# Two heads share one product with the value columns in grouped attention

## The chip, the cores and the metric

The kernel runs on one core of a Trainium2 chip. The time is device microseconds of one execution on that core. The engines named here are TensorE (PE in the profile, with its weight loads as PEld), VectorE (DVE), ScalarE (ACT), GpSimd (POOL) and SyncE (SP); SP and POOL issue the DMA transfers of this kernel, apart from two stores that ACT issues.

## What is computed

Four decoder layers over 256 positions of width 2048, in the order latent attention, sparse attention, sliding-window attention, latent attention. Every layer also has four heads that attend to a memory of 256 rows, a SiLU gate over all head outputs, and one output projection that is added to the residual stream. Data is 32-bit floating point.

The sparse and the window layer are grouped: 32 query heads of 64 columns share 4 key/value heads, eight query heads to each. What the change touches is the last line of their attention, the weighted sum of the values:

```
s = jnp.einsum('bqgjd,bkgd->bgjqk', qb, kb, preferred_element_type=jnp.float32) * scale + bias
...
p = e / (jnp.sum(e, axis=-1, keepdims=True) + jnp.exp(sink - m))
return jnp.einsum('bgjqk,bkgd->bqgjd', p.astype(vb.dtype), vb)
```

These are the window layer's lines; the kernel computes the sparse layer in the same way, with the keys that a query does not select masked out of its weights, and without sinks. All eight query heads j of a group g are multiplied by the same 64 value columns.

## The kernel before

**Numbers in two parts.** A 32-bit operand is split into a high part, rounded to the type that TensorE multiplies, and a low part, the remainder (`split`, line 62: ACT writes the high part, DVE the low part). A product of two such operands is three products: high by high, high by low, low by high. Weights come from HBM through SP's queue into `wr`, are split into `wh` and `wl` (three buffers of each), and are multiplied by activations whose parts are already split. These splits are the bulk of ACT's and DVE's instructions.

**Layers and parts.** A layer's head outputs are made in six parts of 512 columns, in the order 4, 0, 1, 2, 3, 5 (line 844): parts 4 and 5 are memory heads, parts 0 to 3 self heads. In a grouped layer, a part is one key/value group g with its eight query heads. For each part, `project` multiplies the layer's input by the query columns and by the part's gate columns; `attend` runs the heads; the result `y`, gated and split, is multiplied by its rows of the output weights in `w_out` (line 827) one part later, after the next part's projections and attention have been stated.

**Order on the engines.** The program states the work part by part, and a scheduler fixes the order of instructions on each engine when the program is built, moving work of one part between that of another. So on TensorE the small products of a head stand between the large products `acc_q`, `acc_g` (query and gate projections) and `acc_wo` (output projection). Each engine then runs its own list in that order, and waits on semaphores for what other engines deliver.

**One head of a grouped layer** (`Grouped.attend`). Queries are in two blocks b of 128. Block 0 needs keys 0 to 127 only, block 1 all 256. TensorE makes the scores `sp` (lines 786 and 789); DVE adds the bias and takes the maximum (line 447); ACT takes the exponential `e` (line 452) and scales it by the reciprocal of the row sum; TensorE transposes the weights in three blocks of 128x128 into `ptp` (line 427): keys 0 by queries 0, keys 0 by queries 1, keys 1 by queries 1. `split` writes them as 128x384 tiles, the high part `pT` (two buffers) and the low part from the ring `hl` (`part_tile`, line 56, three buffers, which the query projection also uses before its transposes `tr`, line 395). Then come the weighted sums `o` (line 811), with the values `vz` as the stationary operand and the weights as the moving one: key block 0 with 256 columns (both query blocks), key block 1 with 128 columns (query block 1), each three times for the parts. That is six products for one head.

**Two heads in one tile of partitions.** A head has 64 output columns, a stationary operand 128. `vz` holds a group's 64 value columns between columns of zeros, so that an even head takes "values, zeros" and an odd head "zeros, values" and both add into the same 128 partitions of `o`. `o` has 512 columns: heads 0 and 1 of four fill columns 0 to 255, heads 2 and 3 columns 256 to 511. So heads 0 and 2 use the same stationary operand, and heads 1 and 3 the other. After four heads, DVE multiplies `o` by the gate into `yt` (line 415), and `split` writes it into `y`.

**Other users.** Memory attention and latent attention use the `pT` ring too. POOL issues the loads of a group's bias table `bm` (line 775) into a single buffer, and of the memory's keys and values.

Of the kernel before, what the change touches and what calls it, by code (L numbers as in the profile page):

```python
# [8 lines left out]
F32 = mybir.dt.float32  # L9
F32R = mybir.dt.float32r  # L10
# [5 lines left out]
P = 128  # L16
S = 256
# [7 lines left out]
MEMW = 1024  # L25
ST = 2
N_TAB = 384
PQ, AUX, WR = 5, 3, 5


@with_exitstack
def kernel(ctx: ExitStack, tc: tile.TileContext, a: dict, out: bass.AP,
# [13 lines left out]
    def tmp(name, n=512, dt=F32):  # L46
        return wk.tile([P, n], dt, name=name, tag=f"t{n}", bufs=3)
# [6 lines left out]
        return ap.bitcast(F32)  # L54

    def part_tile(dt=F32R):
        return wk.tile([P, 512], dt, name="hl", tag="hl", bufs=3)

    def copy_act(o, i, scale=1.0):
        nc.scalar.activation(o, i, AF.Copy, scale=scale)  # L60
# [1 line left out]
    def split(hi, lo, src):  # L62
        copy_act(hi, src)
        nc.vector.tensor_sub(lo, src, f32(hi))  # L64
# [348 lines left out]
    def gated(y, o, gT, j):  # L413
        yt = tmp("yt")
        nc.vector.tensor_mul(yt, o, gT[:, j:j + 2, :].rearrange("p a b -> p (a b)"))
        y3 = yt.rearrange("p (a b) -> p a b", a=2)
        split(y[:, 0, j:j + 2, :], y[:, 1, j:j + 2, :], y3)
# [73 lines left out]
    def memory_attend(nm, kT, v, qT, gT):  # L491
        y = act.tile([P, 2, 4, S], F32R, name="y", tag="y", bufs=2)
        for h in range(2):
            es = []
            mn, sm = small("mn", 2), small("sm", 2)
            for b in range(2):
                sp = misc("msp")
                qs = slice(b * P, (b + 1) * P)
                seq = [(qT[h][:, u, k, qs], kT[h][:, v_, k, :])
                       for k in range(2) for u, v_ in ((0, 0), (0, 1), (1, 0))]  # L500
                for n_, (l, r_) in enumerate(seq):
                    nc.tensor.matmul(sp[:, :S], l, r_, start=n_ == 0, stop=n_ == len(seq) - 1)
                nc.vector.tensor_reduce(mn[:, b:b + 1], sp[:, :S], AX.X, OP.max, negate=True)
                ms = small("ms", 2)
                nc.vector.tensor_mul(ms[:, :1], mn[:, b:b + 1], nm.col("rstd", b))
                e = wk.tile([P, S], F32, name="e", tag="e", bufs=4)
                nc.scalar.activation(e, sp[:, :S], AF.Exp, bias=ms[:, :1], scale=nm.col("rstd", b),
                                     accum_out=sm[:, b:b + 1])
                es.append(e)
            r = small("rc", 2)  # L510
            nc.vector.reciprocal(r, sm)
            for b in range(2):
                normalized(es[b], r[:, b:b + 1], S)
            tp = weights_T(es, [(0, 0), (1, 0), (0, 1), (1, 1)])
            pH, pL = (wk.tile([P, 512], F32R, name="pT", tag="pT", bufs=2) for z in range(2))
            split(pH, pL, tp)
            o = misc("mo")
            for j in range(2):
                c = (2 * h + j) * P
                seq = [(v[z][:, t, c:c + P], p_[:, t * S:(t + 1) * S])  # L520
                       for t in range(2) for z, p_ in ((0, pH), (0, pL), (1, pH))]
                for n_, (l, r_) in enumerate(seq):
                    nc.tensor.matmul(o[:, j * S:(j + 1) * S], l, r_, start=n_ == 0, stop=n_ == 5)
            gated(y, o, gT, 2 * h)
        return y
# [13 lines left out]
    class Latent:  # L539
# [6 lines left out]
        def first(self):  # L546
            nm, w, j = self.nm, self.w, self.j
            self.cT = [act.tile([P, 2, 4, S], F32R, name=f"cT{c}", tag=f"big{c}")
                       for c in range(4)]

            acc1 = rows_by(nm.at, 16, w, 0, (A_QL, 288), "kva")
            rows_ = act.tile([P, 2, 512], F32, name="ckv", tag="aux", bufs=AUX)
            for t in range(2):
                copy_act(rows_[:, t, :288], acc1[t][:, :288], scale=nm.col("rstd", t))
            acc2 = rows_by(nm.at, 16, w, 0, (A_QL + 288, 288), "kvb")
            ks = small("kss", 2, bufs=2)
            self.kr = act.tile([P, 2, S], F32R, name="kr", tag="kr", bufs=1)
            for t in range(2):
                copy_act(rows_[:, t, 288:], acc2[t][:, :224], scale=nm.col("rstd", t))
                square_sum(ks[:, t:t + 1], rows_[:, t, :])  # L560
                raw = wk.tile([P, S], F32, name="krw", tag="z", bufs=3)
                copy_act(raw[:, :A_ROPE], acc2[t][:, 224:288], scale=nm.col("rstd", t))
                kr = wk.tile([P, 1, A_ROPE], F32, name="krr", tag="krr", bufs=1)
                rope(kr, raw[:, None, :A_ROPE], t, 1)
                hl = wk.tile([P, 2, 2, A_ROPE], F32R, name="krh", tag="krh", bufs=1)
                for d in range(2):
                    split(hl[:, 0, d, :], hl[:, 1, d, :], kr[:, 0, :])
                transposed(lambda i0, i1: self.kr[:, i0:i1, t * P:(t + 1) * P],
                           [hl[:, v_].rearrange("p a b -> p (a b)") for v_ in range(2)])
            kvr = small("kvr", 2, bufs=3)  # L570
            rsqrt_mean(kvr, ks, A_KVL)
            for t in range(2):
                copy_act(rows_[:, t, :], rows_[:, t, :], scale=kvr[:, t:t + 1])
                to_features(self.cT[3], t, rows_[:, t, :], 56 + j * 4)

            sq = wk.tile([P, S], F32, name="cqs", tag="sco0", bufs=1)
            for c in range(6):
                acc = columns_by(nm.at, 16, w, 0, (c * 256, 256), "cq")
                for m in range(2):
                    n = 2 * c + m  # L580
                    z = total(acc[m])
                    s1 = sq if n == 0 else wk.tile([P, S], F32, name="cq1", tag="e", bufs=4)
                    nc.scalar.activation(s1, z, AF.Square)
                    if n:
                        nc.vector.tensor_add(sq, sq, s1)
                    gc = gvec[:, 32 + j * 12 + n:33 + j * 12 + n]
                    hi, lo = (self.cT[n // 4][:, v, n % 4, :] for v in range(2))
                    copy_act(hi, z, scale=gc)
                    nc.vector.scalar_tensor_tensor(lo, z, gc, f32(hi), op0=OP.mult, op1=OP.subtract)
            pr = misc("cqp")  # L590
            for t in range(2):
                nc.tensor.matmul(pr[:, t:t + 1], sq[:, t * P:(t + 1) * P], ones[:, :1], start=True, stop=True)
            s1 = small("cs1", 2)
            nc.vector.tensor_mul(s1, pr[:, :2], nm.rstd)
            s2 = small("cs2", 2)
            nc.vector.tensor_mul(s2, s1, nm.rstd)
            qn = small("qr", 2)
            rsqrt_mean(qn, s2, A_QL)
            qr = small("qx", 2)
            nc.vector.tensor_mul(qr, qn, nm.rstd)  # L600
            self.scale = small("qs", 2, bufs=2), small("qsn", 2, bufs=2)
            for z, sg in zip(self.scale, (1.0, -1.0)):
                nc.vector.tensor_scalar(z, qr, sg * (A_NOPE + A_ROPE) ** -0.5, None, op0=OP.mult)
# [31 lines left out]
        def attend(self, qn, qr, kn, v, gT):  # L635
            y = act.tile([P, 2, 4, S], F32R, name="y", tag="y", bufs=2)
            for h in range(4):
# [12 lines left out]
                        nc.tensor.matmul(sp[:, :S], l, r_, start=n_ == 0, stop=n_ == len(seq) - 1)  # L650
                    return sp
                tp = masked_softmax(score, lambda b, n: caus[:, S - n:], self.scale)
                pT = wk.tile([P, 512], F32, name="pT", tag="pT", bufs=2)
                copy_act(pT[:, :3 * P], tp[:, :3 * P])
                if h % 2 == 0:
                    o = misc("o")
# [7 lines left out]
    class Grouped:  # L664
# [113 lines left out]

        def attend(self, g, q, bm, gT):
            y = act.tile([P, 2, 4, S], F32R, name="y", tag="y", bufs=2)  # L780
            for h in range(8):
                def score(b):
                    sp = misc("sp")
                    qb = q[h // 4][:, h % 4, b * P:(b + 1) * P]
# [14 lines left out]
                    return bs[:, :n]  # L799
                nsk = None if self.sparse else nsink[:, g * 8 + h:g * 8 + h + 1]  # L800
                tp = masked_softmax(score, bias, None, nsk)
                pH, pL = wk.tile([P, 512], F32R, name="pT", tag="pT", bufs=2), part_tile()
                split(pH[:, :3 * P], pL[:, :3 * P], tp[:, :3 * P])
                if h % 4 == 0:
                    o = misc("o")
                c0 = (h // 2 % 2) * S
                v0 = g * P + (64 if h % 2 == 0 else 0)
                for t in range(2):
                    ks = slice(t * S, t * S + S - t * P)
                    for n_, (z, p_) in enumerate(((0, pH), (0, pL), (1, pH))):  # L810
                        nc.tensor.matmul(o[:, c0 + t * P:c0 + S], self.vz[z][:, t, v0:v0 + P], p_[:, ks],
                                         start=h % 2 == t == n_ == 0, stop=h % 2 == t == 1 and n_ == 2)
                if h % 4 == 3:
                    gated(y, o, gT, (h // 4) * 2)
            return y


# [121 lines left out]
```

## Time and profile before

| | |
|---|---|
| median of 3 runs | 2635.22 us (2634.94 to 2639.01) |
| the profiled execution | 2636.8 us, of which 2634.7 are the span of the trace |
| PE, weight loads, DVE, ACT, POOL busy | 2601.2, 2254.7, 1884.1, 1628.8, 57.3 us |
| granted TensorE clock | 0.997 of full speed |
| weighted sums of the sparse layer, first and last start on PE | 1175.5 and 1481.6 us |
| weighted sums of the window layer, the same | 1669.4 and 1974.8 us |

The rows of the timeline give start and length in us, engine, line, operation, the tiles written and read, the shape and the number of instructions that are merged into the row; in brackets the idle time before it and what ended it. Products on PE overlap, and their ends are modelled, so lengths add up to more than the time passed; distances between starts do not. Rows of a group (one line, operation and tile) give the count, the busy time, the mean in ns of one, and the idle time of the engine before them. Rows of the waits give the total, the number and the longest.

### The profile page before, as it was taken

What the parts mean: (1) busy time and instruction counts of PE and PEld (TensorE: products, weight loads), DVE (VectorE), ACT (ScalarE), POOL (GpSimd) and SP (SyncE); (2) the same over time, 40 slices, a digit from 0 to 9 for tenths busy, and PEclk for the clock granted to TensorE, in tenths of its full rate; (3) what the DMA queues carried; (4) which work ended last, traced back from release to release, by engine and by line L of the source; (5) the groups of instructions that cost most, each with busy time, mean ns of one, the idle gap of its engine ahead of it and who ended that gap; (6) DMA issues with size and microseconds to landing.
All of it is one profiled execution on the core that took longest, in us unless ns stands there. A gap on an engine that the chain in (4) does not pass through costs nothing.

```text
span 2634.7 us, 42943 instructions
## 1 busy us (share of the span) xinstructions
PE 2601.2 (99%) x14556; PEld 2254.7 (86%) x14556; DVE 1884.1 (72%) x4171; ACT 1628.8 (62%) x3476; POOL 57.3 (2%) x101
## 2 busy tenths in 40 slices
PE   8999999999999999999999999999999999999998
PEld 7888888888888889888888888888888888888886
DVE  6566656677767685877777776777778767776767
ACT  6455556556656566666666666676666655665655
POOL 1000000000000000000000000000000000000000
PEclk9999999999999999999999999999999999999999
DMA  9889886666557665555555555555555666655764
GB/s 305 279 287 300 281 256 198 166 185 168 169 160 224 192 192 172 167 183 170 173 163 191 188 190 177 173 172 178 189 168 162 205 165 186 165 170 156 226 183 135
DMA packets 456924, 511.70 MB, mean 194 GB/s; under 512 B 69584, under 2 KB 352480, under 8 KB 455552
## 3 DMA queue, kind: packets, MB, share of 16 engines
q1 hardware_dynamic: 443328, 451.75, 56.5%
q0 software_dynamic: 13088, 56.16, 6.6%
q8 instruction: 114, 1.87, 0.3%
q14 instruction: 106, 0.87, 0.1%
q10 hardware_dynamic: 288, 1.05, 0.1%
HBM read 489.91 MB, written 31.56 MB: 198 GB/s over the span
## 4 chain that ended last, share of the span: by engine, by line
PE 97%; DMA 1%; DVE 1%; ACT 0%; issue 0%; SPq 0%; ACTq 0%
PE acc_g L246 14%; PE acc_g L250 7%; PE acc_wo L227 7%; PE acc_wo L228 7%; PE acc_wo L229 7%; PE acc_mq L246 5%; PE acc_mk L246 5%; PE acc_qn L246 3%; PE acc_cq L246 3%; PE acc_mq L250 2%; PE acc_mk L250 2%; PE acc_q L227 2%; PE acc_q L228 2%; PE acc_q L229 2%; PE acc_mv L227 2%; PE acc_mv L228 2%
## 5 line engine op out<-in xcount | busy, mean ns | idle before, releaser
L64 DVE TENSOR_TENSOR wl<-wr,wh 128x512 fp32r<-128x512 f32 (+2 forms) x1776 | 1173.8, 664 | 645.1 <-ACT wh L60 614.2
L60 ACT ACTIVATE wh<-wr 128x512 fp32r<-128x512 f32 (+2 forms) x1776 | 1079.0, 609 | 837.3 <-PE acc_g L246 183.7
L246 PE MATMUL acc_g<-xT,wh 128*128 128x512 f32 x1536 | 489.0, 397 | 0.6 <-DVE z L257 0.6
L250 PEld LDWEIGHTS acc_g<-xT,wl 128*128 128x128 f32 x1536 | 285.2, 188 | 60.7
L250 PE MATMUL acc_g<-xT,wl 128*128 128x256 f32 x1536 | 311.0, 280 | 0.0
L228 PE MATMUL acc_wo<-wl,y 128*128 128x512 f32 x768 | 302.6, 394 | 0.6 <-DVE wl L64 0.5
L229 PE MATMUL acc_wo<-wh,y 128*128 128x512 f32 x768 | 299.1, 390 | 0.0
L246 PEld LDWEIGHTS acc_g<-xT,wh 128*128 128x128 f32 x1536 | 238.1, 189 | 4.8 <-issue 1.1
L227 PE MATMUL acc_wo<-wh,y 128*128 128x512 f32 x768 | 240.4, 393 | 0.7 <-ACT wh L60 0.6
L228 PEld LDWEIGHTS acc_wo<-wl,y 128*128 128x128 f32 x768 | 144.3, 188 | 30.0 <-DVE wl L64 1.4
L229 PEld LDWEIGHTS acc_wo<-wh,y 128*128 128x128 f32 x768 | 144.2, 188 | 28.4
L227 PEld LDWEIGHTS acc_wo<-wh,y 128*128 128x128 f32 x768 | 141.3, 188 | 27.8 <-ACT wh L60 1.0
L246 PE MATMUL acc_mk<-mT,wh 128*128 128x512 f32 x512 | 161.9, 398 | 2.4 <-ACT wh L60 2.4
L246 PE MATMUL acc_mq<-xT,wh 128*128 128x512 f32 x512 | 161.7, 397 | 0.0
L832 DVE TENSOR_TENSOR x<-x,acc_wo 128x512 f32<-128x512 f32 x192 | 125.7, 683 | 7.1 <-PE acc_wo L229 6.8
L246 PE MATMUL acc_qn<-cT,wh 128*128 128x512 f32 x384 | 123.2, 399 | 0.0
L246 PE MATMUL acc_cq<-xT,wh 128*128 128x512 f32 x384 | 120.8, 396 | 0.0
L250 PEld LDWEIGHTS acc_mk<-mT,wl 128*128 128x128 f32 x512 | 96.7, 189 | 23.4 <-DVE wl L64 0.8
L250 PEld LDWEIGHTS acc_mq<-xT,wl 128*128 128x128 f32 x512 | 93.7, 188 | 20.0
L250 PE MATMUL acc_mq<-xT,wl 128*128 128x256 f32 x512 | 102.5, 281 | 0.0
L228 PE MATMUL acc_q<-wl,xT 128*128 128x512 f32 x256 | 102.4, 400 | 0.0
L250 PE MATMUL acc_mk<-mT,wl 128*128 128x256 f32 x512 | 101.7, 280 | 0.0
(280 smaller groups left out, 4438.0 us busy)
## 6 DMA issues: line engine op xcount, KB each, us to landing
wr<-in_w_out_dram SPq DMA_DIRECT2D x192, 512.0 KB, 3.7
wr<-in_w_in_a_dram SPq DMA_DIRECT2D x176, 512.0 KB, 4.1
wr<-in_w_mem_kv_dram SPq DMA_DIRECT2D x128, 512.0 KB, 5.6
wr<-in_w_in_b_dram SPq DMA_DIRECT2D x112, 512.0 KB, 3.5
wr<-in_w_in_c_dram SPq DMA_DIRECT2D x104, 512.0 KB, 3.5
wr<-in_w_uq_dram SPq DMA_DIRECT2D x288, 128.0 KB, 2.6
tab<-flat POOLq DMA_DIRECT2D x8, 1536.0 KB, 11.1
wr<-in_w_in_a_dram SPq DMA_DIRECT2D x32, 288.0 KB, 3.0
```

The source lines that it names most:

```text
L60: nc.scalar.activation(o, i, AF.Copy, scale=scale)
L64: nc.vector.tensor_sub(lo, src, f32(hi))
L227: nc.tensor.matmul(acc[t][:, :n], xh, wh[:, :n], start=first, stop=False)
L228: nc.tensor.matmul(acc[t][:, :n], xh, wl[:, :n], start=False, stop=False)
L229: nc.tensor.matmul(acc[t][:, :n], xl, wh[:, :n], start=False, stop=last)
L246: nc.tensor.matmul(acc[j], wh[:, o:o + P], q[:, :, kt % 4, :], start=kt == 0, stop=False)
L250: nc.tensor.matmul(acc[j][:, 0, :], wl[:, o:o + P], q[:, 0, kt % 4, :], start=False, stop=kt == kts - 1)
L832: nc.vector.tensor_add(xs, xs, acc[t])
```

## The change

In `Grouped.attend` the heads run in the order 0, 2, 1, 3, 4, 6, 5, 7. The weights of two heads that have the same stationary operand (0 and 2, 1 and 3, and so on) are written side by side into one pair of tiles of 128x768, `pT2`, in the order key-and-query block, head, column. After the second head of a pair come its products: key block 0 with 512 columns (two query blocks of two heads), three times, and key block 1 with 256 columns (query block 1 of two heads), three times. `o` now holds its columns in the order query block, head, column, and the gating multiply reads it in that order. `o` is taken after the second head of a pair and not before the first.

Buffers: the `pT` ring has four tiles of 768 columns in place of two of 512, for memory and latent attention too; the `hl` ring has two tiles in place of three, and no longer holds the weights' low parts; the latent layer's `krh` shares the one buffer of `qrs`. The space on chip for descriptors of POOL's transfers is set to 8192 bytes of a partition; it was the default, 16384.

```diff
-PQ, AUX, WR = 5, 3, 5
+PQ, AUX, WR, PT = 5, 3, 5, 4
...
     def part_tile(dt=F32R):
-        return wk.tile([P, 512], dt, name="hl", tag="hl", bufs=3)
+        return wk.tile([P, 512], dt, name="hl", tag="hl", bufs=2)
...
-            pH, pL = (wk.tile([P, 512], F32R, name="pT", tag="pT", bufs=2) for z in range(2))
+            pH, pL = (wk.tile([P, 768], F32R, name="pT", tag="pT", bufs=PT)[:, :512] for z in range(2))
...
-                hl = wk.tile([P, 2, 2, A_ROPE], F32R, name="krh", tag="krh", bufs=1)
+                hl = wk.tile([P, 4, 2, A_ROPE], F32R, name="krh", tag="qrs", bufs=1)[:, :2]
...
-            for h in range(8):
+            for h in (0, 2, 1, 3, 4, 6, 5, 7):
...
-                pH, pL = wk.tile([P, 512], F32R, name="pT", tag="pT", bufs=2), part_tile()
-                split(pH[:, :3 * P], pL[:, :3 * P], tp[:, :3 * P])
-                if h % 4 == 0:
+
+                half, odd = h // 2 % 2, h % 2
+                if half == 0:
+                    pHL = [wk.tile([P, 3, 2, P], F32R, name="pT2", tag="pT", bufs=PT) for z in range(2)]
+                split(pHL[0][:, :, half, :], pHL[1][:, :, half, :],
+                      tp[:, :3 * P].rearrange("p (i c) -> p i c", i=3))
+                if half == 0:
+                    continue
+                if not odd:
                     o = misc("o")
-                c0 = (h // 2 % 2) * S
-                v0 = g * P + (64 if h % 2 == 0 else 0)
+                v0 = g * P + (0 if odd else 64)
                 for t in range(2):
-                    ks = slice(t * S, t * S + S - t * P)
-                    for n_, (z, p_) in enumerate(((0, pH), (0, pL), (1, pH))):
-                        nc.tensor.matmul(o[:, c0 + t * P:c0 + S], self.vz[z][:, t, v0:v0 + P], p_[:, ks],
-                                         start=h % 2 == t == n_ == 0, stop=h % 2 == t == 1 and n_ == 2)
-                if h % 4 == 3:
-                    gated(y, o, gT, (h // 4) * 2)
+                    for n_, (z, p_) in enumerate(((0, 0), (0, 1), (1, 0))):
+                        nc.tensor.matmul(o[:, t * S:], self.vz[z][:, t, v0:v0 + P],
+                                         pHL[p_][:, 2 * t:2 + t].rearrange("p i h c -> p (i h c)"),
+                                         start=odd == t == n_ == 0, stop=odd == t == 1 and n_ == 2)
+                if odd:
+                    j = (h // 4) * 2
+                    yt = tmp("yt")
+                    nc.vector.tensor_mul(yt.rearrange("p (j b c) -> p j b c", j=2, b=2),
+                                         o.rearrange("p (b j c) -> p j b c", b=2, j=2),
+                                         gT[:, j:j + 2, :].rearrange("p j (b c) -> p j b c", b=2))
+                    split(y[:, 0, j:j + 2, :], y[:, 1, j:j + 2, :], yt.rearrange("p (a b) -> p a b", a=2))
...
-    nc = _bacc.Bacc("TRN2", target_bir_lowering=False, num_devices=1)
+    nc = _bacc.Bacc("TRN2", target_bir_lowering=False, num_devices=1,
+                     dynamic_dma_scratch_size=8192)
```

More of the change, by code (lines that the diff above doesn't have):

```diff
@@ L652, in attend @@
                 tp = masked_softmax(score, lambda b, n: caus[:, S - n:], self.scale)
-                pT = wk.tile([P, 512], F32, name="pT", tag="pT", bufs=2)
+                pT = wk.tile([P, 768], F32, name="pT", tag="pT", bufs=PT)[:, :512]
                 copy_act(pT[:, :3 * P], tp[:, :3 * P])
```

## The prediction

> **What bounds the kernel now.** I read the page's first part, then the chain of work that ended last, then the groups of instructions of one line, the waits of TensorE, and last the timeline around the products that the change touches.
>
> ```profile
> span 2634.7 us, 42943 instructions
> PE 2601.2 (99%) x14556; PEld 2254.7 (86%) x14556; DVE 1884.1 (72%) x4171; ACT 1628.8 (62%) x3476; POOL 57.3 (2%) x101
> PE 97%; DMA 1%; DVE 1%; ACT 0%; issue 0%; SPq 0%; ACTq 0%
> 1240.00:1320.00 80.00, 79.23 (x433) 67.42 (x432) 60.85 (x149) 53.95 (x122) 0.89 (x1) 1.00 0.55 171
> 1750.00:1830.00 80.00, 79.53 (x437) 67.88 (x436) 60.65 (x152) 54.43 (x130) 0.89 (x1) 1.00 0.54 172
> ```
>
> TensorE (PE) is the chain for 97% of the span. The last two rows are busy time by stretch, one of the sparse layer and one of the window layer, each about one key/value group long (length, then PE, weight loads, DVE, ACT, POOL, then the granted clock, here 1.00). PE is busy over 79 of 80 us; DVE has 19 us and ACT 26 us to spare. So what the change does to DVE and ACT costs nothing unless it delays something PE waits for, and what it does to PE's stream shows in full.
>
> A busy PE is a modelled number, since the rows of one product overlap those of the next. What a product costs is the distance from its start to the next start:
>
> ```profile
> 1329.63 1.07 PE L227 MATMUL acc_wo<-wh,y 128*128 128x512 f32 x4
> 1330.54 0.39 PE L228 MATMUL acc_wo<-wl,y 128*128 128x512 f32 x1
> ...
> 1356.51 0.28 PE L811 MATMUL o<-pT,vz 128*128 128x256 f32 x1
> 1356.62 0.28 PE L811 MATMUL o<-hl,vz 128*128 128x256 f32 x1
> 1356.74 0.34 PE L811 MATMUL o<-pT,vz 128*128 128x256 f32 x2
> 1356.92 0.28 PE L811 MATMUL o<-hl,vz 128*128 128x128 f32 x1
> 1357.03 0.28 PE L811 MATMUL o<-pT,vz 128*128 128x128 f32 x1
> 1357.14 0.68 PE L227 MATMUL acc_q<-wh,xT 128*128 128x512 f32 x2
> 1357.66 0.40 PE L228 MATMUL acc_q<-wl,xT 128*128 128x512 f32 x1
> ```
>
> (Columns: start, length, engine, line, operation, tiles, shape, count.) Four products of 512 columns take 0.91 us, 0.228 each. A product of 256 columns takes 0.115 (1356.51 to 1356.74 is two); I use 0.117. One head's six products and two of 512 columns take 1.15 us; without the two (0.46) the head costs 0.69 us. Three products of 256 columns are 0.35 of that, so the three of 128 columns take 0.34, 0.11 each: as much as 256 columns. The last two starts, 1356.92 and 1357.03, show the same 0.11. That is the point of the whole case: below 256 columns a product here does not get cheaper, and 512 columns cost twice 256.
>
> **The change, part by part.**
>
> *The products.*
>
> ```profile
> L811 PE MATMUL o<-pT,vz 128*128 128x256 f32 (+1 forms) x256 | 53.4, 266 | 1.7 <-ACT pT L60 1.7
> L811 PE MATMUL o<-hl,vz 128*128 128x256 f32 (+1 forms) x128 | 35.6, 278 | 0.0
> ```
>
> 384 products, 64 heads of six, half of 256 and half of 128 columns: 64 x 0.69 = 44.2 us. Afterwards 32 pairs take three products of 512 and three of 256: 3 x 0.228 + 3 x 0.117 = 1.04 us, 33.2 us in all. The columns streamed are the same; what goes is 192 products and their weight loads, and the gain is that 128 columns paid for 256. The term is -11 us; with each step taken 0.01 us shorter or longer it is -10 to -12. All of it is on PE, so it counts in full. A line of the Trainium skill speaks against this: "TensorE: Matmul & The Clock Gate", Back-to-back issue gap, gives an isolated step of N/2.4 + 2.5 ns, 56 ns at 128 columns and 216 at 512; by it a pair would go from 990 to 975 ns and all pairs would save an estimated 0.5 us. The trace's 0.11 us at 128 columns denies it; it is nearer to the 107 ns that the same page's section on LDWEIGHTS gives for loading 128 columns.
>
> *Order, and the stalls around these products.*
>
> ```profile
> PE o L811 <- ACT pT L60: 1.7, 3, 0.6
> PE ptp L427 <- ACT e L60: 1.4, 3, 0.5
> ...
> 1223.58 0.38 PE L427 MATMUL ptp<-ident,e 128*128 128x128 f32 x2
> 1224.54 0.38 PE L811 MATMUL o<-pT,vz 128*128 128x256 f32 x1 [0.58 <-ACT pT L60]
> 1225.12 0.47 PE L246 MATMUL acc_g<-xT,wh 128*128 128x512 f32 x1 [0.20 <-DVE z L257]
> ...
> 1716.91 0.27 PE L811 MATMUL o<-pT,vz 128*128 128x128 f32 x1
> 1717.65 0.33 PE L427 MATMUL ptp<-ident,e 128*128 128x128 f32 x1 [0.46 <-ACT e L60]
> ```
>
> Three times in the sparse layer the transposes of a head's weights (L427) are followed on PE by the product that needs them; ACT must first copy them out. 0.96 us pass where two transposes need 0.22, then 0.58 where one product needs 0.12: 1.2 us, 3.6 for the three. Three times in the window layer the transposes come before the scaled weights are ready: 0.74 us instead of 0.11, 1.9 for the three. Together 5.5 us. The order of the changed program on each engine is fixed when it is built, so it can be read. Before, these three places have no product between:
>
> ```
> 6383 L427 Matmult ptp_13557<-ident_79,e_13551 128x128 x2
> 6384 L811 Matmult o_13488<-pT_13561,vz_12230 128x256
> ```
>
> Afterwards the fewest between a pair's last transposes and its first product is nine of 512 columns (2.1 us at 0.228), except for the very last pair, with five (1.1 us), where the order before has six. Between a head's last scores and its first transpose stands, with the steps above, 4.6 us of PE work where the window layer stalls for 0.62 us, so that 5.2 would have been enough; afterwards the least is 5.2, once in each layer, then 5.5. So by the order all six stalls go. I count 4.5 of the 5.5, leaving 1 us for a new one somewhere (one place of either kind above); the bounds are 0 and 5.5. Everything PE does before the sparse layer's first projection stands in the same order as before.
>
> *Weights side by side.* ACT and DVE write the same number of 128x384 tiles, now as three runs of 128 with gaps. Nearest rows, runs of 64 with gaps (qrs) against no gaps (mkT):
>
> ```profile
> L60 ACT ACTIVATE qrs<-qrr 128x256 fp32r<-128x256 f32 x16 | 6.5, 406 | 0.0
> L60 ACT ACTIVATE mkT<-zs 128x256 fp32r<-128x256 f32 x32 | 13.2, 413 | 6.1 <-DVE zs L352 6.0
> L415 DVE TENSOR_TENSOR yt<-o,gT 128x512 f32<-128x512 f32 x32 | 22.0, 688 | 4.0 <-PE o L811 4.0
> ```
>
> No cost: 406 against 413 ns. The gating multiply now reads its sums in runs of 128; were its 16 instructions in these layers twice as long, DVE would have 11 us more over eight groups, against 19 us free in each. The sums are read into y, which is multiplied by the output weights only after the next part's projections, so a later pair delays nobody.
>
> *Buffers.* The weights' ring grows from two tiles to four and the first head's tiles are held over two heads; the ring of 512-column tiles (hl) shrinks from three to two but loses the weights' low parts; a rotary temporary shares a buffer used later. Only hl can hurt: each tile is written by ACT and DVE and read by four transposes, and with two tiles ACT's write waits for the transposes of two tiles earlier, with weight splits queued behind it.
>
> ```profile
> L395 PE MATMUL tr<-identr,hl 128*128 128x128 f32 x196 | 23.0, 236 | 0.0
> ```
>
> 196 transposes are 49 tiles, no idle time before them. In the new order the least PE work between a tile's transposes and those two tiles later is 2.6 us, else 3.4 or more. ACT and DVE need 0.47 and 0.48 us for a half tile:
>
> ```profile
> L60 ACT ACTIVATE hl<-acc_q,x 128x256 fp32r<-128x256 f32 x32 | 14.9, 471 | 1.3 <-PE acc_q L229 0.7
> L714 DVE SCALAR_TENSOR_TENSOR hl<-acc_q,x,hl 128x256 fp32r<-128x256 f32 x32 | 15.1, 478 | 2.0 <-ACT hl L60 1.5 <-PE acc_g L250 0.6
> ```
>
> so about 1 us is needed where 2.6 is there. I take 0; the other end is a rival below.
>
> *POOL's descriptor space is halved.* Its queue issues the bias tables of a group:
>
> ```profile
> bm<-tab POOLq DMA_DIRECT2D x8, 1024.0 KB, 6.9
> ...
> 1306.28 0.89 POOL L775 DMA_DIRECT2D bm<-tab  x1 [79.31 <-DVE bs L798]
> 1322.71 0.29 DVE L798 TENSOR_TENSOR bs<-bm,vs 128x128 f32<-128x128 f32 x1
> ```
>
> Issued at 1306.3, landed 6.9 us later, first used at 1322.7: 9.5 us to spare. 0; were a load 10 us slower, each of eight groups would lose half a us.
>
> **Sum.** -11 - 4.5 = -15.5 us. The profiled execution took 2636.8 us for its span of 2634.7; the median of the runs is 2635.2, between the two. From the median: 2619.7, that is 0.6% faster.
>
> **The rivals.**
> 1. The products gain, the stalls don't go. They are where PE's filling work runs short, and the new order only moves that place, at the switch from one half of the gate to the other (the wait for z above) or beside the output products. For it: in this kernel they come back at the same place in each group. Against it: the distances above. 2635.2 - 11 = 2624.
> 2. A product's price goes by its columns, so that pairing changes nothing on PE, and only stalls go: 2635.2 - 4.5 = 2631, or 2634.7 if they stay. Against it: 0.11 us for 128 columns.
> 3. Slower: the two-tile hl ring. If ACT waits at each of 49 tiles and the wh splits behind it come late, PE stands still by the size of the stalls above, 0.6 us each: 29 us, 2635.2 + 29 - 15.5 = 2649. It decides from 15.5 / 49 = 0.32 us a tile. Against it: 2.6 us of PE work for 1 us of ACT and DVE, and no wait of PE on these transposes now.
>
> **Chances.** The forecast 0.61, rival 1 0.26, rival 2 0.06, rival 3 0.07. The measurement tells 0.2% (5.3 us) from no change. The forecast and rival 1 are both faster; rival 2 lies within 0.2% for most of its spread; rival 3 is slower. So faster 0.88, same 0.05, slower 0.07. The range takes in the forecast (2617 to 2623) and rival 1 (2622 to 2627), with the term of the products from -10 to -12 and that of the stalls from +1 to -5.5: 2616 to 2627.
>
> **What would show it.** Right: 192 products of L815, 96 of 512 and 96 of 256 columns, pairs of about 1.04 us from first start to last; a group's stretch about 1.9 us shorter than now, in the sparse and the window layer alike; no row of PE waiting for ACT's pT2 or e; waits before the sparse layer unchanged. Wrong: a step of 512 columns over 0.25 us with these weights; new PE waits on wh or wl in the two layers; DVE or ACT waiting for tr while PE is idle.

## The result and the profile after

The changed kernel takes 2616.65 us (median of 6 runs, 2613.39 to 2619.6); the kernel before takes 2636.04 us beside it (6 runs, 2634.39 to 2639.01). The ratio is 0.9925, with a 95% interval of 0.9912 to 0.9938: about 19.4 us faster, where 15.5 were forecast. The profiled execution took 2616.21 us. The first part of its page and its chain of work that ended last:

```profile
span 2614.0 us, 42540 instructions
PE 2586.5 (99%) x14364; PEld 2238.1 (86%) x14364; DVE 1882.5 (72%) x4171; ACT 1621.6 (62%) x3476; POOL 57.3 (2%) x101
PE 95%; DMA 2%; issue 1%; DVE 1%; ACT 1%; POOL 0%; SPq 0%; ACTq 0%; POOLq 0%
```

TensorE has 192 products fewer (14364 for 14556), still bounds the kernel, and is busy 14.7 us less; VectorE and ScalarE have as many instructions as before. The weighted sums by line and shape (count, busy us, mean ns, idle time before), then the timeline of one pair:

```profile
L815 PE MATMUL o<-pT,vz 128*128 128x512 f32 x96 | 32.6, 400 | 0.3 <-DVE pT L64 0.3
L815 PE MATMUL o<-pT,vz 128*128 128x256 f32 x96 | 16.6, 281 | 0.0
```

```profile
1352.87 1.22 PE L815 MATMUL o<-pT,vz 128*128 128x512 f32 x6
1353.92 0.63 PE L227 MATMUL acc_q<-wh,xT 128*128 128x512 f32 x2
1354.39 0.39 PE L228 MATMUL acc_q<-wl,xT 128*128 128x512 f32 x1
```

From the first product of the pair to the start of the third product behind it are 1.52 us; less two steps of 512 columns (0.46) the pair costs 1.06 us. The forecast was 1.04, and two heads before cost 1.38. The waits of TensorE after (total us, number, longest):

```profile
PE acc_mv L227 <- ACT wh L60: 9.4, 4, 8.4
PE acc_kvb L227 <- ACT wh L60: 2.7, 1, 2.7
PE acc_mk L246 <- ACT wh L60: 1.9, 2, 1.4
PE o L815 <- DVE pT L64: 0.3, 1, 0.3
PE acc_wo L228 <- DVE wl L64: 0.2, 1, 0.2
```

The three waits for ACT's `pT` and the three for `e` are gone. The new one of 0.3 us is at the very last pair. Before, TensorE also waited once at the end of the sparse layer and once at the end of the window layer for the output weights' splits (`acc_wo`, 0.6 and 0.5 us of idle time; the two rows are those quoted under experiment 4, which has them unchanged). Of that 0.2 us are left.

**Where the time went.** I divide every execution at two places, both before or behind everything the change touches on TensorE: the first product of the sparse layer's key/value projection (`acc_kv`) and the first of the last layer's (`acc_kva`). Between them lies what I call the grouped stretch. Busy time by that stretch, before and after (length, then PE, weight loads, DVE, ACT, POOL, granted clock, DMA share, GB/s):

```profile
977.77:2021.35 1043.58, 1038.57 (x5768) 894.17 (x5766) 784.26 (x1817) 682.06 (x1526) 19.07 (x27) 1.00 0.56 176
```

```profile
975.44:2000.71 1025.27, 1024.62 (x5576) 878.61 (x5574) 782.44 (x1817) 675.53 (x1526) 19.05 (x27) 1.00 0.57 180
```

The stretch is 18.3 us shorter. Behind it the two executions take the same time (2634.7 - 2021.35 and 2614.0 - 2000.71, both 613.3). Before it lie 2.3 us of difference (977.77 against 975.44), in a layer of which only buffers have changed. In the eleven profiles of this study the stretch begins between 975.4 and 980.9 us, and in the four other kernels whose head order or buffers alone differ (experiments 4 to 7) between 975.9 and 977.0. TensorE's waits there (the rows of `acc_mv`, `acc_kvb` and `acc_mk`) sum to 15.5 us before and 14.0 after, and to 17.1 in experiment 5 and 15.4 in experiment 7. I take the 2.3 us as a difference from run to run; the forecast that these waits stay as they were can't be judged more closely than that. The stretch is the better ruler for what follows: two kernels below whose edits did nothing came out at 1043.48 and 1043.52, within 0.1 us of the kernel before.

TensorE's idle time in the stretch fell from 5.0 to 0.65 us (length less busy time), its busy time by 13.95.

The rows that were forecast to stay as they were, splits of the weights and the gating multiply, after:

```profile
L60 ACT ACTIVATE pT<-ptp 128x384 fp32r<-128x384 f32 x64 | 31.2, 487 | 16.7 <-PE ptp L427 16.2
```

```profile
L64 DVE TENSOR_TENSOR pT<-ptp,pT 128x384 fp32r<-128x384 f32 x64 | 35.5, 555 | 2.8 <-ACT pT L60 2.8
L821 DVE TENSOR_TENSOR yt<-o,gT 128x512 f32<-128x512 f32 x16 | 11.0, 688 | 1.5 <-PE o L815 1.4
```

and the two splits before, where they wrote without gaps (ACT's high part, then DVE's low part):

```profile
L60 ACT ACTIVATE pT<-ptp 128x384 fp32r<-128x384 f32 x64 | 31.1, 486 | 20.5 <-PE ptp L427 20.0
```

```profile
L64 DVE TENSOR_TENSOR hl<-ptp,pT 128x384 fp32r<-128x384 f32 x64 | 35.5, 554 | 0.6 <-ACT pT L60 0.6
```

The multiply took 688 ns before too. Runs of 128 with gaps cost nothing.

### The profile page after: what moved, and what is told of

It is laid out like the page before. It is cut to its first block, busy times and chain, and to the rows that moved or that the text cites. A ratio compares the mean times of both kernels' runs of the same rounds, so it can differ in the third digit from the quotient of the medians.

```text
span 2614.0 us, 42540 instructions
## 1 busy us (share of the span) xinstructions
PE 2586.5 (99%) x14364; PEld 2238.1 (86%) x14364; DVE 1882.5 (72%) x4171; ACT 1621.6 (62%) x3476; POOL 57.3 (2%) x101
## 3 DMA queue, kind: packets, MB, share of 16 engines
q8 instruction: 113, 1.85, 0.3%
## 4 chain that ended last, share of the span: by engine, by line
PE 95%; DMA 2%; issue 1%; DVE 1%; ACT 1%; POOL 0%; SPq 0%; ACTq 0%; POOLq 0%
PE acc_g L246 14%; PE acc_g L250 7%; PE acc_wo L227 7%; PE acc_wo L228 7%; PE acc_wo L229 7%; PE acc_mq L246 5%; PE acc_mk L246 4%; PE acc_qn L246 3%; PE acc_cq L246 3%; PE acc_mq L250 2%; PE acc_q L228 2%; PE acc_q L229 2%; PE acc_q L227 2%; PE acc_mk L250 2%; PE acc_qn L250 2%; PE acc_cq L250 2%
```

## The experiments

The theory was: 11 us come from the width of the products, because 128 columns cost what 256 do, and the rest from the six stalls, which the new order removes. What it did not say is which part of the change makes the new order: the pairing, the order of the heads, or the buffers. The rivals are those of the prediction.

**1. The pairs kept, the products narrow again.** Everything of the change stays, weights side by side included, but each product of 512 columns is made as two of 256 and each of 256 as two of 128.

```diff
-                        nc.tensor.matmul(o[:, t * S:], self.vz[z][:, t, v0:v0 + P],
-                                         pHL[p_][:, 2 * t:2 + t].rearrange("p i h c -> p (i h c)"), ...
+                        pf = pHL[p_][:, 2 * t:2 + t].rearrange("p i h c -> p (i h c)")
+                        for s0 in range(0, w, step):        # w 512, 256; step = (256, 128)[t]
+                            nc.tensor.matmul(o[:, t * S + s0:t * S + s0 + step], self.vz[z][:, t, v0:v0 + P],
+                                             pf[:, s0:s0 + step], ...
```

> The changed kernel with its products cut back: same head order, same paired tiles and buffers, but each product of 512 columns is issued as two of 256 and each of 256 as two of 128, 12 products a pair as before the change. Theory (128 columns cost as much as 256, 0.11 us): a pair goes from 1.04 back to about 1.36 us, 32 pairs cost 10 to 11 us, so 2627 us against 2616.7 of the changed kernel and still 9 us under before, because the stalls are a matter of the order. Rival (a product's price goes by its columns): no change from the changed kernel, 2617. Second rival (the stalls went because of the wide products): 2635, as before.

Measured: 2627.8 us (7 runs) beside 2634.84, ratio 0.9974 (0.9963 to 0.9984). The stretch, and one pair in the timeline:

```profile
980.86:2017.15 1036.29, 1035.16 (x5767) 894.07 (x5766) 785.49 (x1817) 678.03 (x1526) 19.07 (x27) 1.00 0.58 178
```

```profile
1204.07 1.50 PE L819 MATMUL o<-pT,vz 128*128 128x256 f32 x12
1205.40 0.67 PE L227 MATMUL acc_q<-wh,xT 128*128 128x512 f32 x2
1205.92 0.40 PE L228 MATMUL acc_q<-wl,xT 128*128 128x512 f32 x1
```

The pair costs 1.85 - 0.46 = 1.39 us: the two heads of before. Between it and the change lie 1036.29 - 1025.27 = 11.0 us of the stretch, 10.5 of them busy time of TensorE; 32 pairs by 1.39 - 1.06 give 10.6. Width alone is therefore worth some 10.5 us. The rest is in the waits, which differ a little because the order does: experiment 1 waits four times for the gated sums at the output projection, which the change does not.

```profile
PE acc_wo L227 <- ACT y L60: 1.1, 4, 0.3
```

What is left against the kernel before, 7.3 us, has nothing to do with the width.

**2 and 3. Nine products per pair, in two ways.** In experiment 2 only the 256-column products are cut, in experiment 3 only those of 512. The number of products and of weight loads is the same, and so are the columns.

```diff
+                    step = (512, 128)[t]        # experiment 2: 3 x 512 and 6 x 128
...
+                    step = (256, 256)[t]        # experiment 3: 9 x 256
```

> The changed kernel with only its second kind of product cut: 512 columns for key block 0, but two products of 128 columns in place of each 256 for key block 1, 9 products a pair. Theory (below 256 columns nothing gets cheaper, 512 costs twice 256): nearly the whole loss of the 12-product version, 32 x 3 x 0.11 = 10 us, so 2626 to 2627. Rival (each product and weight load has a fixed price): half the loss, since half of the removed products are back, 2622. Rival (price by columns): 2617.

> The changed kernel with only its first kind of product cut: two products of 256 columns in place of each of 512 for key block 0, 256 columns for key block 1, again 9 products a pair. Theory: 6 x 0.117 + 3 x 0.117 = 1.05 us a pair against 1.04, no loss, 2616 to 2618. Rival (fixed price per product): half the loss, 2622. Together with the version of 512 and 128 columns this tells which half of the change bears the gain, at the same number of products.

Measured: experiment 2 2630.17 us (11 runs), ratio 0.9978 (0.997 to 0.9987); experiment 3 2618.67 us (5 runs), ratio 0.9933 (0.9921 to 0.9946). The stretch of experiment 2, then of experiment 3:

```profile
978.61:2015.45 1036.84, 1035.19 (x5671) 889.60 (x5670) 785.98 (x1817) 677.98 (x1526) 19.06 (x27) 1.00 0.59 178
```

```profile
976.53:2002.86 1026.33, 1025.70 (x5672) 883.32 (x5670) 781.74 (x1817) 676.13 (x1526) 19.06 (x27) 1.00 0.59 180
```

A price by columns makes these two equal, and so does a fixed price per product; they differ by 10.5 us, 9.5 of them busy time of TensorE. Experiment 2 stands where experiment 1 does, with 96 products fewer; experiment 3 stands 1.1 us from the full change, with 96 more. Nearly all the gain of the width is that no product has 128 columns any more. Between 256 and 512 columns there is next to nothing: 0.0 us of busy time from experiment 1 to 2, 1.1 from experiment 3 to the change. The whole time of experiment 2 is 3 to 4 us over what was expected and 2.4 over experiment 1; its stretch is only 0.6 longer, so most of that lies outside the stretch and is not explained.

**4. The buffers alone.** The kernel before, its heads and products untouched, with the change's buffers: four weight tiles of 768 columns that hold high and low parts, two `hl` tiles, `krh` shared, POOL's descriptor space halved.

```diff
-        return wk.tile([P, 512], dt, name="hl", tag="hl", bufs=3)
+        return wk.tile([P, 512], dt, name="hl", tag="hl", bufs=2)
...
-                pH, pL = wk.tile([P, 512], F32R, name="pT", tag="pT", bufs=2), part_tile()
+                pH, pL = (wk.tile([P, 768], F32R, name="pT", tag="pT", bufs=PT)[:, :512] for z in range(2))
```

> The kernel before with the change's buffers alone: weights' ring of four tiles of 768 columns for both parts, the other ring of two tiles, the shared rotary buffer and the smaller descriptor space; heads and products as before. In its order of instructions on TensorE the products that followed their transposes at once (three places in the sparse layer) now have eight products of 512 columns between, and the least work from a head's scores to its transposes in the window layer is 6.1 us in place of 4.6. Theory (the six stalls of 5.5 us are a matter of this order, which the buffers alone already change): 2636 - 5.5 = 2630.5, with no row of TensorE waiting for the weights or for e. Rival (the pairing removes the stalls, buffers do nothing): 2636. Rival of the prediction (the ring of two tiles delays ACT): over 2636.

Measured: 2629.76 us (10 runs), ratio 0.9978 (0.9969 to 0.9988). The stretch, then the waits of TensorE in the grouped layers and at their ends:

```profile
976.38:2013.93 1037.55, 1036.26 (x5768) 893.43 (x5766) 782.62 (x1817) 677.51 (x1526) 19.09 (x27) 1.00 0.59 178
```

```profile
PE acc_wo L227 <- ACT wh L60: 0.6, 1, 0.6
PE acc_wo L228 <- DVE wl L64: 0.5, 1, 0.5
```

No row of `pT` or `e` is left: all six stalls go without any pairing, and the stretch loses 6.0 us. Of these, 3.7 are idle time and 2.3 busy time of the same products. That is how a stall looks in modelled lengths: in the row that the prediction quotes, 0.96 us pass from the start of the two transposes to the next product. They need 0.22, so 0.74 are lost, but only 0.58 are drawn as idle time; the rest is in the drawn length of the transposes, 0.38. The two rows of `acc_wo` stand in the kernel before as well. The buffers of the change cost nothing and bring a third of its gain.

**5 and 7. The head order alone, the longer ring alone.** Experiment 5 is the kernel before with its heads in the order 0, 2, 1, 3, 4, 6, 5, 7 (and the marks of a sum's start and end moved to the first and last product of four heads). Experiment 7 is the kernel before with four `pT` tiles for two, the low parts still in `hl`; like experiment 6, it has POOL's descriptor space halved to make room.

```diff
-            for h in range(8):
+            for h in (0, 2, 1, 3, 4, 6, 5, 7):        # experiment 5
...
-                pH, pL = wk.tile([P, 512], F32R, name="pT", tag="pT", bufs=2), part_tile()
+                pH, pL = wk.tile([P, 512], F32R, name="pT", tag="pT", bufs=4), part_tile()        # experiment 7
```

> The kernel before with the head order 0, 2, 1, 3 alone; products and buffers as before (the start and stop marks of the sums are set once for four heads). Its order on TensorE still has three products right behind their transposes and 4.6 us from scores to transposes in the window layer. Theory (order of the heads does nothing): the stretch from the sparse layer's first projection to the last layer's stays at 1043.6 us (within 0.5), and the waits for the weights (1.7 us, 3 times) and for e (1.4, 3) stay. Rival (taking heads 0 and 2 one after the other removes the stalls): 1038.

> The kernel before with the weights' ring of four tiles of 512 columns in place of two, the low parts still in the shared ring of three (descriptor space smaller, as in the change). Its order has the same stalled places as before. Theory: the grouped stretch stays at 1043.6 us (within 0.5) with all six waits. Rival (the longer ring is what helps): 1038.

Measured, one run each: 2635.89 and 2634.88 us, beside 2631.25 for one run of the kernel before. Single runs here scatter by several us, so the stretch decides. The stretch of experiment 5, then two of the waits of experiment 7:

```profile
976.97:2020.45 1043.48, 1038.46 (x5768) 894.15 (x5766) 784.26 (x1817) 683.72 (x1526) 19.10 (x27) 1.00 0.56 177
```

```profile
PE o L811 <- ACT pT L60: 1.7, 3, 0.6
...
PE ptp L427 <- ACT e L60: 1.4, 3, 0.5
```

Neither moves the stretch (1043.48 here, 1043.52 in the other), and both keep the six stalls: experiment 5 has the same two rows. By tile and shape, TensorE's list of products in the stretch is in both traces that of the kernel before, product for product; in experiments 4 and 6 it is another. So neither the head order nor the number of `pT` tiles made the stalls.

**6. The low parts out of `hl`.** The kernel before with four `pT` tiles of 512 columns that take high and low parts; `hl` keeps its three.

```diff
-                pH, pL = wk.tile([P, 512], F32R, name="pT", tag="pT", bufs=2), part_tile()
+                pH, pL = (wk.tile([P, 512], F32R, name="pT", tag="pT", bufs=4) for z in range(2))
```

> The kernel before with one thing of the buffers: the weights' low parts are written into the weights' ring, which has four tiles of 512 columns, and no longer into the other ring, which keeps three tiles (descriptor space smaller, to make room). In its order no product follows its transposes at once any more, and the window layer has 6.1 us. Theory (the low parts' sharing a ring with the projection's tiles is what set the stalled places): the grouped stretch falls by the 5.5 to 6 us of the buffers alone, 1043.6 to 1038. Rival (it is the four tiles, or the two-tile ring): no change.

Measured: 2631.73 us (one run). The stretch, the waits, and one of the places in the timeline:

```profile
976.07:2016.25 1040.18, 1037.27 (x5767) 893.79 (x5766) 783.28 (x1817) 679.03 (x1526) 19.09 (x27) 1.00 0.56 177
```

```profile
PE acc_wo L227 <- ACT wh L60: 2.4, 5, 0.6
```

```profile
1729.25 0.40 PE L789 MATMUL sp<-kd,qS 128*128 128x256 f32 x2
1730.18 1.02 PE L227 MATMUL acc_wo<-wh,y 128*128 128x512 f32 x3 [0.54 <-ACT wh L60]
```

The six old stalls are gone, and experiment 7, with four tiles but the low parts left in `hl`, keeps them; so it was the ring shared by the query projection's tiles and the weights' low parts that set the bad order. But the stretch gains only 3.4 us: three new stalls have come in the window layer, at the output weights. (Of the five waits, one of 0.6 us is in the kernel before too, and one is 0.15 us.) There 0.93 us pass where two score products need 0.23 (2 x 0.117), a loss of 0.70 each, and the three products behind them take 0.86 us (to a start at 1731.04) for 0.69. Three times both are 2.6 us, and 6.0 - 2.6 is the 3.4 that was measured. This is what rival 1 foresaw, at another place: stalls that move.

**9. The change with three `hl` tiles.** The two-tile ring was the one thing of the change that could hurt. Here it is given its third tile back.

```diff
-        return wk.tile([P, 512], dt, name="hl", tag="hl", bufs=2)
+        return wk.tile([P, 512], dt, name="hl", tag="hl", bufs=3)
```

> The changed kernel with the ring of 512-column tiles at three again. Asked: what the ring of two costs the changed kernel, and whether three beats it. Rival of the prediction (two tiles delay ACT): the grouped stretch falls below the changed kernel's 1025.3 us, by up to 0.3 us a tile. Theory (ACT's wait is covered; the ring's length acts through the order alone): in its order the least from scores to transposes is 4.7 us at one place, where 4.6 gave 0.62 us of stall, and else 5.2 or more, so 1025 to 1027 and 2616 to 2619, the same as the changed kernel.

Measured: 2620.75 us (5 runs) beside 2636.54, ratio 0.9945 (0.9931 to 0.9958). The stretch, and one of three like places:

```profile
975.58:2003.40 1027.82, 1025.10 (x5576) 878.46 (x5574) 782.44 (x1817) 676.25 (x1526) 19.09 (x27) 1.00 0.59 179
```

```profile
1237.36 0.40 PE L229 MATMUL acc_wo<-wh,y 128*128 128x512 f32 x1
1238.52 1.02 PE L227 MATMUL acc_wo<-wh,y 128*128 128x512 f32 x3 [0.77 <-ACT wh L60]
```

The stretch is 2.5 us longer than with two tiles, where the same as the changed kernel was expected; the expectation had looked at the distances from scores to transposes alone. At 1237.36, 1393 and 1877 us, 1.16 us pass where one product needs 0.23. Three stalls of 0.93 are 2.8 us; the change's own short wait for `wl` (0.2 us) is missing here. ScalarE is not too busy for these splits: at the first place it is idle for 1.36 us, and starts the split at 1237.84, just behind the end of TensorE's last product (1237.36 and 0.40). More buffer is slower here: with three tiles the scheduler may put work in an order that leaves the output weights' splits late, with two it may not. TensorE's list of products differs from that of the change; that the order is all of the difference was not tested apart, and why the scheduler chose it was not traced.

**8. Is it the weight load that holds the 128-column product?** In experiment 1's kernel, the even pairs' products (all but the last two of each pair) load only the 64 stationary columns that hold values. The odd pair goes first, so that the sums of all 128 partitions have been started. Columns streamed and number of products stay.

```diff
-            for h in (0, 2, 1, 3, 4, 6, 5, 7):
+            for h in (1, 3, 0, 2, 5, 7, 4, 6):
...
+                        m = P if odd or (t == 1 and n_ == 2) else 64
...
+                            nc.tensor.matmul(o[:m, t * S + s0:t * S + s0 + step], self.vz[z][:, t, v0:v0 + m],
+                                             pf[:, s0:s0 + step], ...
```

> The version cut back to 12 products a pair, with the odd pair of heads first; the even pair's products, but for the last two, load only the 64 columns of values and leave out the 64 of zeros, so that they write partitions 0 to 63. Asked: what holds a product of 128 columns at 0.11 us. Theory (the load of 128 stationary columns, one before each product): with 64 stationary columns the products of 128 step by about 0.06 us, those of 256 stay at 0.117; 16 pairs x 4 x 0.05 us = 3 us less in the grouped stretch than the 1036.3 us of the version with 128 stationary columns. Rival (a least price of any product of its own): 0.11 us again, 1036.

Measured: 2626.05 us (one run). One even pair in the timeline, to be compared with that of experiment 1:

```profile
1198.89 1.33 PE L820 MATMUL o<-pT,vz 128*64 128x256 f32 x12
1200.06 0.68 PE L227 MATMUL acc_q<-wh,xT 128*128 128x512 f32 x2
1200.58 0.39 PE L228 MATMUL acc_q<-wl,xT 128*128 128x512 f32 x1
```

The pair costs 1.69 - 0.46 = 1.23 us for 1.39: four products of 128 columns are 0.04 us cheaper each. In the single records of this pair their starts lie 0.060 us apart, those with 128 stationary columns 0.112, and the 256-column products stay at 0.117 with either. So the floor of 0.11 us follows the stationary columns, not the streamed ones. The Trainium skill's page "TensorE: Matmul & The Clock Gate", section on LDWEIGHTS, puts the time of a weight load, in ns, at its columns divided by 1.2: an estimated 53 ns for 64 and 107 for 128. The steps of 0.060 and 0.112 us lie 5 to 7 ns above these, so this trace agrees. The stretch is 1034.9 us, 1.4 less than in experiment 1, where 3 was expected and sixteen even pairs by 0.16 would be 2.6. TensorE's waits for the output weights, 1.5 us in two places, are new there, but experiment 1's four waits for `y` (1.1 us) are gone, and counted by the distances of starts either cost about 2.3 us. So the waits don't account for it, and the missing 1.2 us stay open.

**No version here beats the change:** experiments 3 (2618.67) and 9 (2620.75) come nearest to its 2616.65. Narrower weight loads have nothing to give to products of 256 columns, which keep 0.117 us with 64 stationary columns; those of 512 were not tried.

## Why the prediction was right, and where it was off

The forecast was 2619.7 us, faster; 2616.65 lies 3 us below it, inside the range near its lower end. The bounds of the two terms, -12 and -5.5, reach -17.5 together, and the stretch lost 18.3: the term of the stalls (first row below) went beyond its bound, and the 1.3 us of the second row were in no term. That the median stayed inside the range, by 0.65 us and with two of its six runs below 2616, is partly luck. In the stretch the account closes along a chain of kernels, each differing from the next by one part of the change:

| from, to | stretch, us | difference | predicted |
|---|---|---|---|
| before, buffers alone (4) | 1043.6, 1037.6 | -6.0 | 0, with -4.5 put down to the new order |
| buffers alone, pairs with narrow products (1) | 1037.6, 1036.3 | -1.3 | 0 |
| narrow products, the change | 1036.3, 1025.3 | -11.0 | -11 |
| together | 1043.6, 1025.3 | -18.3 | -15.5 |

*The products.* Right in size and reason. 10.5 to 11.0 us were measured for the 11 predicted; a pair costs 1.06 for 1.04. The price of 0.11 us for a narrow product is a mean over a head's block: in the prediction's rows the two products from 1356.74 take 0.18 us, not 0.23, and the two wide ones from 1357.14 take 0.52, not 0.46. The sum over the block with the wide ones behind it, which the prediction used, takes in both. Rival 2, a price by columns, falls with experiments 2 and 3. The rule of the Trainium skill that was weighed there ("TensorE: Matmul & The Clock Gate", Back-to-back issue gap), a figure for an isolated product by which the pairs would save an estimated 0.5 us, does not hold for this stream: 10.5 were saved. The Trainium skill's section on LDWEIGHTS on the same page, which the prediction only found nearer, is borne out by experiment 8 (steps of 0.112 and 0.060 us).

*The stalls.* Right that all six go, and that the very last pair, with five products between, is the tightest place: it waits 0.3 us. The size was short. The prediction found 5.5 us, counted 4.5 to leave room for a new stall, and 6.0 came. The three waits for `z` of 0.20 us stand right behind the stalled products in its own quoted rows; they went too, and 5.5 + 0.6 is 6.1. They were read as a rival's evidence and not as part of the stall. The two waits for the output weights at the ends of the layers, 1.1 us of idle time, were not counted; they shrink to 0.2 in the change.

*The cause of the new order* was not named by the prediction, which took the order as built. It set the buffers at 0 and looked only for harm in them. The runs show that the buffers alone make the order (experiment 4), by way of the ring that two users shared (6) and, it seems, of its two tiles (9 against the change, and 6 against 4, which differ in the tiles' width and in `krh` too). The head order does nothing to the stalls (5), and they go without any pairing; pairing with the old buffers was not tried.

*Rival 1*, stalls that only move, did not happen in the change but does in its neighbours, experiments 6 and 9, at the output weights. A chance of about one in four was not too much. *Rival 3*, that two `hl` tiles would stop TensorE, is denied with the sign turned round: two tiles are 2.5 us faster than three.

*Beside the products.* Strided writes, the gating multiply and POOL's descriptor space were each counted at nothing, and the rows above and experiments 4 and 7, which have the space halved, agree.

*The groups.* The forecast that a group would be 1.9 us shorter in both layers alike holds only on average. By the starts of `acc_q`, groups that took 80.2 us in the sparse layer take 78.7 and 77.2 one after the other, and 79.5 in the window layer become 78.9 and 77.3.

*What stays open.* The 1.3 us between experiments 4 and 1 are nearly all busy time of TensorE (1036.26 and 1035.16) for the same products. Waits do not explain them: TensorE is idle for 1.3 us of the stretch in experiment 4 and for 1.1 in experiment 1, and counted by the distances of starts its waits cost about 2.4 us in either (two by 1.2, four by 0.6). Pairs make half as many changes between these small products and the large ones, and a change may cost a little; this was only argued, not tried. And some 1 to 2 us of the 19.4 lie outside the stretch, in the first layer, where the runs differ among themselves by more than that.

## What to carry to other kernels

Price a product by its distance to the next start, not by its columns: with 128 stationary columns nothing below 256 streamed columns gets cheaper here, so put work side by side until 256 are reached, and expect little from 512. When a change touches buffers, test the buffers alone: a ring that two users share ties their order together, and undoing that, with one tile fewer in the ring, was worth 6 of 18 us here without any of the intended work. Read the order of the built program for stalls, and count with each stall the shorter waits that stand right behind it.

## What was not expected of the hardware

A product with 64 stationary and 128 streamed columns starts 0.060 us before the next, where 128 stationary columns take 0.112 and 256 streamed columns 0.117 with either (experiment 8). Buffers, which no engine pays for, moved the stretch both ways: 6.0 us faster with fewer `hl` tiles and a ring of their own for the weights (experiment 4), and 2.5 us slower when the third `hl` tile came back (experiment 9).
